# Two decoder layers: five steps of each mixer moved one feature later in TensorE's order

## The chip, the cores and the metric

One NeuronCore of a Trainium2 chip runs the whole kernel in one launch. The metric is the device time of one execution in microseconds; the time before is the median of three runs. The profile shown is of one execution, and its times count from the first instruction.

## What is computed

Two layers on 256 tokens of width 1024, all in float32. In each layer the tokens are projected, four mixers of width 256 work side by side, their results are joined and projected back, and a layer norm and a gated feed-forward follow. Cut to what matters here:

```python
def hybrid_mixer(x, w_in, b_forget, ...):
    z = x @ w_in
    aq, ak, av, bq, bk, bv, bf, cu, cv, dp = jnp.split(z, IN_SPLITS, axis=-1)
    ya = moba_attention(partial_rotary(aq), partial_rotary(ak), av)
    log_f = jax.nn.log_sigmoid(bf + b_forget)
    yb = forgetting_attention(bq, bk, bv, log_f)
    yc = causal_spatial_gating(gelu(cu), gelu(cv), ...)
    yd = multiscale_pool(dp, pool_w, pool_scale)
    return concatenate([ya, yb, yc, yd]) @ w_o

def forgetting_attention(q, k, v, log_f):
    c = jnp.cumsum(log_f, axis=-1)
    logits = q @ k.T * scale + c[..., :, None] - c[..., None, :]
    p = softmax(where(kpos <= qpos, logits, -inf))
    return p @ v
```

With 256 tokens and blocks of 256 the first attention is a plain causal softmax attention behind a rotation of the first 16 dimensions of each head. Both attentions have four heads of 64, worked on in pairs: index i = 0 and 1.

## The kernel before, in words

**Numbers.** A product of two float32 matrices is made of three products of rounded parts (float32r): high times high, high times low, low times high. So each weight is loaded (DMA on SyncE's queue, half a megabyte at a time), cast to its high part on ScalarE (L134, `wh`) and reduced to its low part on VectorE (L136, `wl`). This is called a split. `weights` (L142) asks for the splits of the unit that TensorE needs and of those up to `reach` units after it; there are 12 buffers for high parts, 10 for low ones.

**The mixer's steps.** `tokens` makes the values of both attentions, the gating branch and the forget gates with tokens on partitions. `feature(i, c)` (L453) makes a block of 128 features for all 256 tokens from one unit of weights: 8 x 3 products. Features 0 are the gating's, 1 the pooling's; 2 and 4 are queries and keys (c = 0, 1) of the first attention's head pairs 0 and 1, 3 and 5 those of the forgetting attention. Then:

- `forget_gates` (L397): a chain of small operations on VectorE that ends in the copies into `nlx`. `cumulate` (L418) sums them over the tokens by four products with a triangle (L420, L421); ScalarE copies rows of the sum into `fq` and `fk`.
- `rotary(i, z)` (L468): ScalarE copies the feature (`zrot`), VectorE multiplies it by cosines (`qk`) and shuffles the copy (`swp`), GpSimd multiplies that by sines (L477), VectorE adds it into `qk`.
- `forget(i, z)` (L482): ScalarE copies queries and keys into `fq` and `fk`. `pick_heads` (L202) prepares the other rows of these on GpSimd (L206, L207) for a head pair.
- `pooling`, `pool_means`: sums over windows on GpSimd. `pool_out` (L574): products (L577), ScalarE scales, and `result` splits into `yh` and `yl`.
- `scores(mx, i)` (L491): products of queries and keys (L507) of mixer mx (0 the first attention, from `qk`; 1 the forgetting one, from `fq` and `fk`) and their softmax: two reductions a head on VectorE into `pr`, exponentials on ScalarE, reciprocals and products on VectorE.
- `turned(mx, i)` (L521): transposes of `pr` on TensorE (L527), copied by ScalarE into `pt`. `values(mx, i)` (L533): products with the values (L539), then `result` (L319).
- `project(kt, ...)` (L585): the joint projection (L595 to L597) of one block of 128 features of the result.

**What sets the order.** TensorE's order is the order of the program, written out in L599 to L660 (manual schedule). The other engines' orders are set by a scheduler, when the program is built: by priority, earlier lines first, filling idle time with whatever is ready, splits above all. Each engine then works its list in order. The steps are `urgent` (L264): their instructions get a higher priority, and those on VectorE and ScalarE are queued behind the last recorded instruction of the urgent steps before:

```python
def urgent(f):
    def g(*a, **k):
        with ExitStack() as es:
            es.enter_context(tc.high_priority(offset=URGENT))
            for e in ORDERED:
                if recent[e] is not None:
                    es.enter_context(tc.issue_after(recent[e].ins))
            return f(*a, **k)
    return g
```

All recorded instructions are issued from one helper, so the profile shows them as L257, told apart by their tiles.

Of the kernel before, what the change touches and what calls it, by code (L numbers as in the profile page):

```python
# [24 lines left out]
SCALE = HD ** -0.5  # L25
# [31 lines left out]
def hybrid_block(ctx, tc, x, xT, wA1, wA3, wZ, wO, wU, wD, lnp, vecs, sguwT, sgub, scalep, convp, poolw, consts, out):  # L57
# [18 lines left out]
    mask = cst[:, CW_MASK:CW_MASK + 256]  # L76
    neghalf = cpool.tile([P, 4], F32, name="neghalf")

# [1 line left out]
    stream = []  # L80
    index = {}

# [25 lines left out]
    behind = [None]  # L108
# [37 lines left out]
            split_one()  # L146
        return units[i]

# [1 line left out]
    xTh = cpool.tile([P, NKT, S], F32R, name="xTh")  # L150
    xTl = cpool.tile([P, NKT, S], F32R, name="xTl")
    x_sb = [None, None]
# [15 lines left out]
        nc.scalar.copy(xTh[:, ks, :], xv)  # L168
        nc.vector.tensor_sub(xTl[:, ks, :], xv, xTh[:, ks, :].bitcast(F32))

    # the array's clock rises with a few microseconds of work: products of zeros while the first loads run
    idle = apool.tile([P, 512], F32, tag="w2", name="idle", bufs=W2).bitcast(BF16)[:, 0:512]
    nc.vector.memset(idle, 0.0)
    warm = psum()
    first = load_xT(0, 1)
# [16 lines left out]
        for o, e in ((CW_WIN, CW_TRI), (CW_TRI, CW), (CW_COS, CW_WIN)):  # L192
            nc.sync.dma_start(cst[:, o:e], consts[:, o:e])

    # forgetting attention: q k + (c_q - c_k) / SCALE as one product over a head's 64 rows and, in the other 64,
    # (1 / SCALE at the head's row | -c) times (-c | -1 / SCALE at the head's row)
    nlx = cpool.tile([P, 2, P], F32, name="nlx")
    nc.gpsimd.memset(nlx, 0.0)
    fq = [cpool.tile([P, S], F32, name=f"fq{h}") for h in range(2)]
# [47 lines left out]
    recent = {"vector": None, "scalar": None}  # L247

    class Recorded:
        """An engine whose last instruction is kept, for the stages that follow to queue behind it."""  # L250

        def __init__(self, name):
            self.name, self.engine = name, getattr(nc, name)
# [19 lines left out]

    @urgent
    def layer_norm(m, acc, ln, final):
        """x = LN(alpha x + acc) of 128 tokens; returns what transposes half of it for the products to come."""
        r = x_sb[m]
        last = final and m == 1
        spans = THREE if last else HALVES
        step = 256 if last else 512  # L280
        st = apool.tile([P, 4, 6], F32, tag="lnst", name="lnst")
        for o, w in spans:
            vector.scalar_tensor_tensor(r[:, o:o + w], r[:, o:o + w], ALPHA, acc[o][:, :w],
                                        op0=ALU.mult, op1=ALU.add)
            for c in range(o, o + w, step):
                vector.bn_stats(st[:, c // step, :], r[:, c:c + step])
        mv = apool.tile([P, 4], F32, tag="mv", name="mv")
        vector.bn_aggr(mv[:, 0:2], st[:, :DM // step, :].rearrange("p a b -> p (a b)"))
        nc.gpsimd.tensor_scalar(mv[:, 2:3], mv[:, 1:2], LN_EPS, None, op0=ALU.add)  # L289
        nc.gpsimd.tensor_tensor(mv[:, 3:4], mv[:, 2:3], neghalf[:, 0:1], op=ALU.pow)  # L290
        for n in range(2):
            ns = slice(512 * n, 512 * n + 512)
            vector.scalar_tensor_tensor(r[:, ns], r[:, ns], mv[:, 0:1], ln[:, 0, ns],
                                           op0=ALU.subtract, op1=ALU.mult)
        for i, (o, w) in enumerate(spans):
            ns = slice(o, o + w)
            behind[0] = vector.scalar_tensor_tensor(r[:, ns], r[:, ns], mv[:, 3:4], ln[:, 1, ns],
                                                    op0=ALU.mult, op1=ALU.add)
            if final:
                (nc.sync, nc.scalar)[i % 2].dma_start(out[m * P:(m + 1) * P, ns], r[:, ns])  # L300

        @urgent
        def turn(n):
            tp = psum()
            for k in range(4):
                nc.tensor.transpose(tp[:, k * P:(k + 1) * P], r[:, 512 * n + k * P:512 * n + (k + 1) * P], ident)
            tv = tp.rearrange("p (k t) -> p k t", k=4)
            ks, ms = slice(4 * n, 4 * n + 4), slice(m * P, (m + 1) * P)
            scalar.copy(xTh[:, ks, ms], tv)
            vector.tensor_sub(xTl[:, ks, ms], tv, xTh[:, ks, ms].bitcast(F32))  # L310

        return turn

    def mixer(l, norm2):
# [2 lines left out]
        yT = {}  # L317

        def result(kt, src):  # L319
            """Splits a block of the mixers' joint result, features on partitions, for the projection."""  # L320
            yh = apool.tile([P, S], F32R, tag="yh", name="yh", bufs=YB)
            yl = apool.tile([P, S], F32R, tag="yl", name="yl", bufs=YB)
            scalar.copy(yh, src)
            vector.tensor_sub(yl, src, yh.bitcast(F32))
            yT[kt] = (yh, yl)

        # tokens on partitions: values of both attentions, the gating branch, the forget gates
        V, VN = [], []
        zf = apool.tile([P, 2, 4], F32, tag="zf", name="zf")

# [59 lines left out]
            for r in held + tokens("A1", (1,)) + tokens("A3", (1,)):  # L390
                token_results(*r)

        # log_sigmoid(z) = min(z, 0) - 2 atanh(w / (2 + w)), w = exp(-|z|)
        zz = zf.rearrange("p m h -> p (m h)")

        @urgent
# [20 lines left out]
        @urgent  # L417
        def cumulate():  # L418
            ps = psum()
            nc.tensor.matmul(ps[:, :S], nlx[:, 0, :], tri, start=True, stop=False)  # L420
            nc.tensor.matmul(ps[:, P:S], nlx[:, 1, :], tri[:, 0:P], start=False, stop=True)  # L421
            for hh in range(2):
                o = HD - HD * hh
                scalar.copy(fk[hh][o:o + 32, :], ps[o:o + 32, :S])
                scalar.copy(fq[hh][o + 32:o + HD, :], ps[o + 32:o + HD, :S])

        # gating: mix the tokens of each chunk, features on partitions
        gate_u = {}

        @urgent  # L430
# [30 lines left out]
                nc.tensor.matmul(a, wh, xTl[:, k, :], start=False, stop=False)  # L461
                nc.tensor.matmul(a, wl, xTh[:, k, :], start=False, stop=(k == NKT - 1))  # L462

        # attention: queries and keys, scores, weights transposed, values, transposed result
        att = {}

        @urgent
# [21 lines left out]

        @urgent  # L490
        def scores(mx, i):  # L491
            """Heads 2i, 2i+1 of mixer mx: negated logits, masked, and their softmax over the keys."""
            t = att[mx, i]
            nm = apool.tile([P, 2, 2], F32, tag="nm", name="nm")
            sm = apool.tile([P, 2, 2], F32, tag="sm", name="sm")
            spans = ((0, P), (P, 2 * P))
            t["pr"] = []
            for hh in range(2):
                if mx == 0:
                    rows = slice(hh * HD, (hh + 1) * HD)  # L500
                    q, k = t["qk"][rows, 0, :], t["qk"][rows, 1, :]
                else:
                    q, k = fq[hh], fk[hh]
                ps = psum()
                pr = apool.tile([P, 384], F32, tag="pr", name="pr", bufs=4)
                for m, (o, n) in enumerate(spans):
                    nc.tensor.matmul(ps[:, o:o + n], q[:, m * P:(m + 1) * P], k[:, 0:n], start=True, stop=True)  # L507
                for m, (o, n) in enumerate(spans):
                    vector.tensor_tensor_reduce(out=pr[:, o:o + n], in0=ps[:, o:o + n], in1=mask[:, 2 * P - n:],
                                                   op0=ALU.add, op1=ALU.min, scale=-SCALE, scalar=3e38,  # L510
                                                   accum_out=nm[:, hh, m:m + 1])
                for m, (o, n) in enumerate(spans):
                    scalar.activation(pr[:, o:o + n], pr[:, o:o + n], AF.Exp, bias=nm[:, hh, m:m + 1],
                                         scale=-1.0, accum_out=sm[:, hh, m:m + 1])
                vector.reciprocal(sm[:, hh, :], sm[:, hh, :])
                for m, (o, n) in enumerate(spans):
                    vector.tensor_scalar(pr[:, o:o + n], pr[:, o:o + n], sm[:, hh, m:m + 1], None, op0=ALU.mult)
                t["pr"].append(pr)
# [43 lines left out]

        @urgent
        def pool_means():
            """A window's sum less the window's size times the token; the size divides after the product."""
            po = pool["po"]
            nc.gpsimd.tensor_mul(d["scale"], d["scale"], means)
            for i, total in enumerate(pool["sums"]):
                rows, g = slice(i % 2 * HD, (i % 2 + 1) * HD), i // 2
                nc.gpsimd.tensor_mul(total[rows, 16:32], total[rows, 16:32], start[rows, g, :])  # L570
                nc.gpsimd.tensor_sub(po[rows, g, :], total[rows, 16:], po[rows, g, :])  # L571
# [27 lines left out]
        both = (0, 1)  # L599
# [12 lines left out]
        if norm2 is None:  # L612
            load_x()
        gating()
        cumulate()
        feature(3, 1)
        forget(0, 3)
        scores(0, 0)
        feature(4, 0)
        scores(1, 0)  # L620
        feature(4, 1)
        turned(0, 0)
        pick_heads(1)
        rotary(1, 4)
        pool_out()
        feature(5, 0)
        values(0, 0)
        turned(1, 0)
        feature(5, 1)
        forget(1, 5)  # L630
        values(1, 0)
        scores(0, 1)
        reach[0] = HIGHS - 1
        project(4, both)
        scores(1, 1)
        project(5, both)
        turned(0, 1)
# [242 lines left out]
```

## Time and profile before

| | |
|---|---|
| median of 3 runs | 586.87 us (585.36 to 587.61) |
| profiled execution, first to last instruction (span) | 583.9 us; its time as the runs count it is not recorded |
| mean granted TensorE clock | 0.990 of full |
| TensorE products busy | 563.0 us (96%) |
| VectorE, ScalarE, GpSimd busy | 445.5 (76%), 323.9 (55%), 80.9 us (14%) |
| HBM read | 105.16 MB |

PE is TensorE, DVE VectorE, ACT ScalarE, POOL GpSimd, SP SyncE. A TensorE that is busy 96% of the span can only be made faster where it stands still or runs at a lower clock; both are found by stage, not in the sums. The first mixer's features run from about 25 to 72 us, the second's from about 311 to 357 us.

### The profile page before, as it was taken

The numbers are of one execution on the slowest core, as the hardware profiler recorded it, in microseconds if no ns is written. First come the engines' busy times: TensorE is split into PE (matmuls) and PEld (weight loads), VectorE is DVE, ScalarE is ACT, GpSimd is POOL, SyncE is SP. The second block draws the span as 40 slices with busy tenths as digits, with TensorE's granted clock in tenths as the row PEclk, the third lists the DMA queues.
The fourth block names the chain that finished last, engine by engine and source line by source line (L and its number), as shares of the span: only waits on it lengthen the run. The fifth ranks groups of instructions, "written<-read, shape, count | busy, mean of one in ns | idle before, by whom it ended". The sixth has DMA issues, their size and how long they took to land.

```text
span 583.9 us, 10273 instructions
## 1 busy us (share of the span) xinstructions
PE 563.0 (96%) x3962; PEld 515.2 (88%) x3962; DVE 445.5 (76%) x781; ACT 323.9 (55%) x539; POOL 80.9 (14%) x104
## 2 busy tenths in 40 slices
PE   7997999999999999999999989999999999999994
PEld 4996877899899999999789978779999999999994
DVE  4688985988877777678898868488886777767756
ACT  5774972386655555555548468435764555555420
POOL 2186431100000000000117730020000000000002
PEclk9998999999999999999999989999999999999998
DMA  8976871485555554445468624318656655544101
GB/s 284 336 259 211 282 269 70 160 309 185 199 194 181 181 184 176 146 150 177 150 207 312 226 73 133 134 36 319 222 183 186 201 188 180 182 148 152 63 1 72
DMA packets 31473, 106.88 MB, mean 183 GB/s; under 512 B 3776, under 2 KB 5184, under 8 KB 30912
## 3 DMA queue, kind: packets, MB, share of 16 engines
q1 hardware_dynamic: 31136, 105.83, 53.8%
q8 instruction: 31, 0.51, 0.4%
q10 hardware_dynamic: 288, 0.39, 0.2%
q14 instruction: 18, 0.15, 0.1%
HBM read 105.16 MB, written 1.05 MB: 182 GB/s over the span
## 4 chain that ended last, share of the span: by engine, by line
PE 77%; POOL 8%; DVE 8%; DMA 3%; issue 2%; ACT 1%; SPq 0%; POOLq 0%; DVEq 0%; ACTq 0%
PE ps L706 13%; PE ps L705 13%; PE ps L704 13%; PE ps L740 6%; PE ps L738 6%; PE ps L739 6%; DVE x L257 2%; PE ps L595 2%; PE ps L597 2%; PE ps L596 2%; DVE wl L136 2%; PE ps L340 2%; PE ps L341 1%; DVE lnst L257 1%; POOL po L571 1%
## 5 line engine op out<-in xcount | busy, mean ns | idle before, releaser
L136 DVE TENSOR_TENSOR wl<-wr,wh 128x1024 fp32r<-128x1024 f32 (+2 forms) x185 | 225.3, 1225 | 64.2 <-PE ps L706 41.2
L134 ACT CAST wh<-wr 128x1024 fp32r<-128x1024 f32 (+2 forms) x185 | 191.1, 1043 | 116.1 <-PE ps L705 58.1
L704 PE MATMUL ps<-xTh,wh 128*128 128x256 f32 x640 | 179.6, 281 | 0.0
L706 PE MATMUL ps<-xTh,wl 128*128 128x256 f32 x640 | 179.3, 280 | 0.0
L705 PE MATMUL ps<-xTl,wh 128*128 128x256 f32 x640 | 179.3, 280 | 0.0
L705 PEld LDWEIGHTS ps<-xTl,wh 128*128 128x128 f32 x640 | 120.6, 188 | 1.0
L704 PEld LDWEIGHTS ps<-xTh,wh 128*128 128x128 f32 x640 | 120.4, 188 | 1.0
L706 PEld LDWEIGHTS ps<-xTh,wl 128*128 128x128 f32 x640 | 120.6, 188 | 0.0
L257 DVE SCALAR_TENSOR_TENSOR cva<-ps,conv,cva 128x255 f32<-128x255 f32 (+1 forms) x176 | 84.5, 480 | 18.8 <-ACT cva L257 15.6
L257 ACT ACTIVATE cva<-ps,conv 128x256 f32<-128x256 f32 x88 | 49.5, 562 | 43.8 <-DVE cva L257 42.2
L738 PE MATMUL ps<-wh,gh 128*128 128x512 f32 (+1 forms) x198 | 73.3, 370 | 0.0
L740 PE MATMUL ps<-wh,gl 128*128 128x512 f32 (+1 forms) x198 | 73.2, 370 | 0.0
L739 PE MATMUL ps<-wl,gh 128*128 128x512 f32 (+1 forms) x198 | 73.1, 369 | 0.0
L289 POOL TENSOR_SCALAR mv<-mv 128x1 f32<-128x1 f32 x8 | 6.3, 782 | 423.5 <-DVE mv L257 423.5
L460 PE MATMUL ps<-xTh,wh 128*128 128x256 f32 x192 | 56.5, 294 | 0.0
L461 PE MATMUL ps<-xTl,wh 128*128 128x256 f32 x192 | 55.1, 287 | 0.0
L462 PE MATMUL ps<-xTh,wl 128*128 128x256 f32 x192 | 55.1, 287 | 0.0
L740 PEld LDWEIGHTS ps<-wh,gl 128*128 128x128 f32 x198 | 37.2, 188 | 6.9
L739 PEld LDWEIGHTS ps<-wl,gh 128*128 128x128 f32 x198 | 37.3, 188 | 5.8
L738 PEld LDWEIGHTS ps<-wh,gh 128*128 128x128 f32 x198 | 37.2, 188 | 5.7
L460 PEld LDWEIGHTS ps<-xTh,wh 128*128 128x128 f32 x192 | 37.7, 197 | 0.8 <-issue 0.7
L461 PEld LDWEIGHTS ps<-xTl,wh 128*128 128x128 f32 x192 | 37.6, 196 | 0.1
(126 smaller groups left out, 735.9 us busy)
## 6 DMA issues: line engine op xcount, KB each, us to landing
wr<-in_wU_dram SPq DMA_DIRECT2D x88, 512.0 KB, 3.8
wr<-in_wD_dram SPq DMA_DIRECT2D x44, 512.0 KB, 3.4
wr<-in_wZ_dram SPq DMA_DIRECT2D x24, 512.0 KB, 4.9
wr<-in_wO_dram SPq DMA_DIRECT2D x16, 512.0 KB, 4.4
lnp<-in_lnp_dram SPq DMA_DIRECT2D x4, 1024.0 KB, 5.5
wr<-in_wA_dram SPq DMA_DIRECT2D x7, 512.0 KB, 3.5
wr<-in_wA_dram SPq DMA_DIRECT2D x4, 520.0 KB, 4.4
x<-in_x_dram SPq DMA_DIRECT2D x4, 256.0 KB, 4.7
```

What stands on the lines that cost most here:

```text
L134: nc.scalar.copy(h[:, ps], raw[:, ps])
L136: nc.vector.tensor_sub(lo[:, ps], raw[:, ps], h[:, ps].bitcast(F32))
L257: ins = getattr(self.engine, op)(*a, **k)
L460: nc.tensor.matmul(a, wh, xTh[:, k, :], start=(k == 0), stop=False)
L461: nc.tensor.matmul(a, wh, xTl[:, k, :], start=False, stop=False)
L462: nc.tensor.matmul(a, wl, xTh[:, k, :], start=False, stop=(k == NKT - 1))
L704: nc.tensor.matmul(a, wh, xTh[:, k, :], start=(k == 0), stop=False)
L705: nc.tensor.matmul(a, wh, xTl[:, k, :], start=False, stop=False)
L706: nc.tensor.matmul(a, wl, xTh[:, k, :], start=False, stop=(k == NKT - 1))
L738: nc.tensor.matmul(a, gh[:, t], h[:, c], start=(j == 0), stop=False)
L739: nc.tensor.matmul(a, gh[:, t], lo[:, c], start=False, stop=False)
L740: nc.tensor.matmul(a, gl[:, t], h[:, c], start=False, stop=(j == NPAIR - 1))
```

## The change

In both mixers `cumulate` and `scores(0, 0)` move behind `feature(4, 0)`; `rotary(1, 4)` and `pool_out` come before `scores(1, 0)`, which moves behind `feature(4, 1)`; `pick_heads(1)` stays behind `scores(1, 0)`; `turned(0, 0)` moves behind `feature(5, 0)`, `values(0, 0)` and `turned(1, 0)` behind `feature(5, 1)` and `forget(1, 5)`, and `values(1, 0)` behind `project(4)`. The order of the features and projections among themselves stays. The diff's other parts only remove comments.

```diff
@@ -612,26 +612,26 @@
         if norm2 is None:
             load_x()
         gating()
-        cumulate()
         feature(3, 1)
         forget(0, 3)
+        feature(4, 0)
+        cumulate()
         scores(0, 0)
-        feature(4, 0)
-        scores(1, 0)
         feature(4, 1)
-        turned(0, 0)
-        pick_heads(1)
         rotary(1, 4)
         pool_out()
+        scores(1, 0)
+        pick_heads(1)
         feature(5, 0)
+        turned(0, 0)
+        feature(5, 1)
+        forget(1, 5)
         values(0, 0)
         turned(1, 0)
-        feature(5, 1)
-        forget(1, 5)
-        values(1, 0)
         scores(0, 1)
         reach[0] = HIGHS - 1
         project(4, both)
+        values(1, 0)
         scores(1, 1)
         project(5, both)
         turned(0, 1)
```

## Rows read from the trace of the kernel before

**Rows 1.** Waits of TensorE in the first mixer (19 to 100 us): engine line, releaser: us in total, times, longest
```profile
PE ps L420 <- issue: 3.4, 1, 3.4
PE ps L507 <- DVE qk L257: 1.0, 2, 0.7
```

**Rows 2.** Windows, TensorE alone: stretch, length, PE busy (instructions), granted clock, DMA share, GB/s
```profile
27.61:30.45 2.84, 2.84 (x27) 1.00 0.96 330
49.60:54.21 4.61, 4.61 (x27) 0.63 0.42 133
339.41:343.87 4.46, 4.46 (x27) 0.62 0.23 71
```

**Rows 3.** Timeline of TensorE, second mixer: start us, us, what, count [idle before <-releaser]
```profile
338.55 0.93 PE L507 MATMUL ps<-qk 64*128 64x128 f32 x8 [2.55 <-DVE qk L257]
...
343.87 1.47 PE L507 MATMUL ps<-fk,fq 128*128 128x128 f32 x8
...
353.27 0.88 PE L527 MATMUL ps<-cst,pr 128*128 128x128 f32 x6
...
356.91 0.87 PE L539 MATMUL ps<-pt,v 128*64 128x256 f32 x8
```

**Rows 4.** Chain of work that ended last, first mixer: start us, us, what
```profile
30.21 1.68 POOL gv L374
...
52.03 1.99 POOL swp L477
```

**Rows 5.** Timeline of TensorE, first mixer
```profile
54.87 0.93 PE L507 MATMUL ps<-qk 64*128 64x128 f32 x8 [0.66 <-DVE qk L257]
...
58.71 1.58 PE L507 MATMUL ps<-fk,fq 128*128 128x128 f32 x8
...
68.49 1.26 PE L527 MATMUL ps<-cst,pr 128*128 128x128 f32 x6
72.49 0.87 PE L539 MATMUL ps<-pt,v 128*64 128x256 f32 x8
```

**Rows 6.** Windows, VectorE alone: stretch, length, DVE busy (instructions), granted clock, DMA share, GB/s
```profile
54.03:73.55 19.52, 18.32 (x48) 1.00 0.86 288
```

**Rows 7.** Windows of the splits on VectorE (L136) alone, same columns
```profile
54.03:69.26 15.23, 8.47 (x7) 1.00 0.84 273
54.03:73.55 19.52, 9.69 (x8) 1.00 0.86 288
```

**Rows 8.** Waits of ScalarE, 60 to 110 us, columns as in rows 1
```profile
ACT wh L134 <- PE ps L597: 12.1, 3, 8.8
```

**Rows 9.** Timeline of ScalarE, second mixer
```profile
342.62 0.37 ACT L257 COPY fk<-ps 64x256 f32<-64x256 f32 x1
343.01 1.05 ACT L134 CAST wh<-wr 128x1024 fp32r<-128x1024 f32 x1
```

**Rows 10.** Timeline of VectorE, second mixer
```profile
346.06 0.90 DVE L257 TENSOR_SCALAR pr<-pr,sm 128x128 f32<-128x128 f32 x2
...
348.01 0.28 DVE L257 CUSTOM_DVE_ANT_0 pr<-ps,cst 128x128 f32<-128x128 f32 x1
...
350.43 0.55 DVE L257 TENSOR_SCALAR pr<-pr,sm 128x128 f32<-128x128 f32 x2
...
352.54 0.69 DVE L257 TENSOR_TENSOR qk<-ps,cst 128x512 f32<-128x512 f32 x1 [0.42 <-ACT zrot L257]
...
353.15 0.75 DVE L257 STREAM_SHUFFLE swp<-zrot 128x512 f32<-128x512 f32 x1
355.37 0.69 DVE L257 TENSOR_TENSOR qk<-qk,swp 128x512 f32<-128x512 f32 x1 [1.47 <-POOL swp L477]
355.98 0.76 DVE L257 TENSOR_TENSOR yl<-yd,yh 128x256 fp32r<-128x256 f32 x2
```

**Rows 11.** Timeline of GpSimd: L477 of rotary(1, 4) in the first and the second mixer
```profile
70.69 2.14 POOL L477 TENSOR_TENSOR swp<-swp,cst 128x512 f32<-128x512 f32 x1 [6.28 <-DVE swp L257]
...
354.05 1.29 POOL L477 TENSOR_TENSOR swp<-swp,cst 128x512 f32<-128x512 f32 x1 [5.25 <-DVE swp L257]
```

## The prediction

> **What bounds the kernel now.** I read the page of the profile first: in a span of 583.9 us TensorE is busy for 563.0. Its order is written out by hand, so only two things can be won by moving steps: time in which it stands still, and time in which it runs at half clock. The view of TensorE's waits over the first mixer shows two standstills: 3.4 us at `cumulate` (L420) and 1.0 us in two waits for `qk` at `scores` [rows 1]. The windows show the second loss: a whole `feature` takes 2.84 us at a granted clock of 1.00, but the one after each long wait took 4.61 and 4.46 us, at 0.63 and 0.62, so part of it ran at 1.2 instead of 2.4 GHz: 1.8 and 1.6 us lost [rows 2]. The timeline of the second mixer shows one long wait, 2.55 us for `qk` at `scores(0, 0)` [rows 3]; at `cumulate` there is none. All standstills and slow stretches of both mixers together are 3.42 + 0.66 + 0.34 + 2.55 + 1.8 + 1.6 = 10.4 us, the most that could be gained.
>
> The chain of waits then tells who is late. In the first mixer it runs over GpSimd from 30.21 us to the `sin` product L477, which begins at 52.03 and takes 1.99, and from there over VectorE's sum into `qk` to `scores(0, 0)` at 54.87 [rows 4, 5]. So the wait at `cumulate` is not what the chain hangs on: had TensorE not waited there, it would have waited for `qk`. Behind that sum VectorE, which works in order, is full: from 54.03 to 73.55 it is busy 18.32 of 19.52 us, and 9.69 of these are eight splits of weights (L136) [rows 6, 7].
>
> **The change, part by part.** No instruction is added or removed. The features keep their order, and with it every weight load on SyncE's queue and the place where each split is asked for; the splits are far ahead (ScalarE's casts wait up to 8.8 us for TensorE to free a buffer [rows 8]), so an earlier feature finds its weights. I cost the loads at nothing; if that cover were gone, one late weight would hold TensorE for a cast and a split, 1.05 + 1.21 = 2.3 us [rows 7, 9].
>
> *Part 1, `cumulate` and `scores(0, 0)` behind `feature(4, 0)`.* First mixer: the 3.4 us at `cumulate` go, since two features now stand there. But without that wait and the slow stretch `feature(3, 1)` and `cumulate`, which only change places, are done at 54.87 - 0.66 - 3.42 - 1.8 = 49.0, and `feature(4, 0)` at 51.8. `scores(0, 0)` is reached then and stands until 54.87, because nothing on GpSimd or VectorE ahead of `qk` is touched. The wait is 3.0 us long, near that of before, and a half-clock stretch behind it is likely again. What is won at this point is one feature, 2.84 us. Second mixer: the hole of 2.55 us is filled with `feature(4, 0)`, and `scores(0, 0)` begins at 338.55 - 2.55 + 2.84 = 338.84, without a wait. Won here: the hole, 2.55 us, and the 1.6 us of clock.
>
> *Part 2, `rotary(1, 4)` and `pool_out` ahead of `scores(1, 0)`.* Here is the price. Each urgent step queues its VectorE and ScalarE work behind that of the step before. Today the softmax of `scores(1, 0)` follows that of `scores(0, 0)`; after the change the product, shuffle, wait for GpSimd's L477 and sum of `rotary(1, 4)`, and the two `yl` of `pool_out`, stand between: 0.69 + 0.75 + 0.69 + 0.76 us and the GpSimd trip [rows 10]. `turned(1, 0)`, which needs the result, is now followed on TensorE by `scores(0, 1)` and the whole projection.
>
> When does TensorE reach `turned(1, 0)`? Before, from the start of `scores(1, 0)` to `turned(1, 0)` stand 9.78 us in the first mixer and 9.40 in the second [rows 3, 5]. After the change the same steps and `feature(5, 1)` (2.84) lie between the end of `scores(0, 0)` (0.93 after its start) and it: 55.8 + 12.62 = 68.4, and 339.8 + 12.24 = 352.0. The last copy into `fk` ends at 342.99 in the second mixer [rows 9], 4.4 us behind the start of `scores(0, 0)`; `feature(4, 1)` and `pool_out` take about as long, so `scores(1, 0)` finds its inputs.
>
> When are the weights of `scores(1, 0)` ready? First mixer, by VectorE's own sum: 18.32 - 9.69 = 8.63 us of work that must be done from 54.03 on, plus the two `yl` (0.76) that came after it: 9.4. With each split 1.21 us and k of them let in: 54.03 + 9.4 + 1.21 k. Today seven were let in before the last normalisation of `scores(1, 0)`, which ends at 69.26 [rows 7]; I take 7, which gives 71.9. Second mixer: the softmax of `scores(0, 0)` ends at 346.96; product and shuffle 1.4; L477; sum 0.69; `yl` 0.76; then 2.97 from the first reduction to the last normalisation (348.01 to 350.98) [rows 10]. L477 took 1.29 us with VectorE idle and 2.14 with a split beside it [rows 11]; splits will fill this wait, so I take 2.1: 354.9.
>
> So TensorE waits some 3 us at `turned(1, 0)` in each mixer. Its second half then takes 0.44 us (half of 0.88 [rows 3]), and `scores(0, 1)` starts at 72.3 and 355.3. The same point of work before, with `values(1, 0)` not yet done, was 72.49 + 0.34 = 72.8 and 356.91. Gain: 0.5 and 1.6 us. Bounds: in the first mixer k from 5 (gain 2.9) to 8 with 1.2 us of idle VectorE as today (loss 2.0); in the second from 3.5 (the cast of 1.05 us not ahead of the exponentials [rows 9], L477 at 1.29) to 0.4 (one more split).
>
> About L477 the Trainium skill (SBUF — State Buffer, section "SBUF: two separate sides") says that VectorE with two SBUF inputs and GpSimd hold a shared port by an exclusive lock, so that the later one blocks for the whole instruction. By that an L477 behind a split would take up to 1.29 + 1.21 = 2.5 us, an estimate, and the second mixer would gain 1.2 instead of 1.6 and the sum be 586.9; the measured 2.14 is below it, and I keep 2.1.
>
> *Part 3, the clock.* Waits of 3.42 and 2.55 us were each followed by half clock; those of 0.66 and 0.34 were not. The waits at `turned(1, 0)` come in two pieces with transposes between, and in the first mixer a slow stretch behind `scores(0, 0)` makes TensorE arrive 1.7 us later and the wait shorter. I count one half-clock stretch for the two mixers, 1.7 us, with 0 and 3.4 as ends.
>
> *The rest.* `values(0, 0)` and `turned(0, 0)` find their inputs (in the second mixer the softmax ends at 346.96 and `turned(0, 0)` is reached at about 347.4; in the first it has the same distance). `values(1, 0)` behind `project(4)` has its transposes copied during that projection. `scores(0, 1)` no longer waits for `qk` (0.34, already counted). `pick_heads(1)` on GpSimd moves behind L477 in program order; its next reader, `scores(1, 1)`, is over 3 us away. From 0 to 1 us if a PSUM buffer is late at `project(4)`; I take 0.
>
> Sum: 0.5 + 1.6 - 1.7 = 0.4 us faster. The profiled execution's span is 583.9, the median of the runs 586.87, 3.0 above it; I take the difference from the median: **586.5 us**. Own range of this case, from its bounds: 584.0 to 589.5.
>
> **Rivals.** *Faster: the softmax is in time.* If few splits are let in (k = 5) and no cast stands ahead of the exponentials, the gains are 2.9 and 3.5, the waits at `turned(1, 0)` fall to about 1 us and no half clock follows: 580.5 at its end, 582.5 as its middle. For it: in the second mixer L477 did run at 1.29, with VectorE idle beside it. Against it: VectorE's 94% in the first.
>
> *Slower: the softmax of `scores(1, 0)` behind rotary's GpSimd trip becomes the bound.* If eight splits and today's idle stand ahead of it in the first mixer (-2.0), one split more in the second (+0.4), and both waits end in half clock (-3.4): 587 + 5 = 592 at its end, 590.5 in its middle. It decides once TensorE stands at `turned(1, 0)` for over about 4 us in the first mixer. For it: VectorE has no slack there. Against it: TensorE then has two more features behind it.
>
> *The change does nothing in the end:* `qk` bounds the first mixer on both sides and the second's gain goes into one half-clock stretch; 586.9, inside the forecast's band.
>
> **Chances.** What a measurement of this kernel can tell from no change is about 0.5%, 2.9 us. Faster by more 0.30 (the first rival and the forecast's good end), within it 0.45 (the forecast 0.38, the last rival 0.07), slower by more 0.25. As both outer cases hold more than a tenth, the range reaches to their middles: 581.5 to 590.5.
>
> **What would show it.** Right: TensorE's wait at L420 gone in the first mixer, a wait of about 3 us at L507 for `qk` in its place; no wait at L507 in the second mixer; new waits at L527 for `pr`, 1.5 to 3.5 us in each; the `pr` rows of `scores(1, 0)` on VectorE behind the two `yl` of `pool_out`. Wrong: `pr` ready before TensorE comes (gain then up to the hole itself), `qk` of the first mixer ready well before 54, or waits at `project(4)` for a PSUM buffer.

## The result, and the profile after

The changed kernel takes 595.12 us in the median of 4 runs (592.79 to 595.47), the kernel before 586.31 (now four runs, 585.36 to 587.61). By the medians it is slower by 8.8 us, and outside the predicted range. The ratio used from here on is formed from the single runs and not from the medians: 1.0141, with an interval of 1.0124 to 1.0158. The profiled execution has a span of 593.2 us, 9.3 above that of before.

The page of the changed kernel, its head: TensorE is busy for 2.3 us longer than before (563.0 us then); the other 7.0 of the 9.3 us are time in which it stands.

```profile
PE 565.3 (95%) x3962; PEld 514.7 (87%) x3962; DVE 446.2 (75%) x781; ACT 324.6 (55%) x539; POOL 81.6 (14%) x104
```

**Where it stands.** (In what follows, pair 0 and pair 1 are the two head pairs of the first attention, and half clock is a stretch with a granted clock of 0.50.) Call the stretch from the first product of `gating` (L443) to the first transposes of the layer norm (L306) a mixer stage; everything that the change moves lies in it. The first stage took 56.27 us before and takes 61.11 now (46.54 to 107.65), the second 53.50 and 55.83 (338.17 to 394.00): 4.84 + 2.33 = 7.2 of the 9.3 us. From the first stage's end to the second's start (230.5) and from the second's end to the last instruction (199.2) nothing differs by over 0.1. The other 2.1 us lie ahead of the first stage, where no step is moved (the last section comes back to them).

Waits of TensorE in the changed kernel, first mixer (44 to 110 us), then second (335 to 395), in the columns of [rows 1]:

```profile
PE ps L539 <- ACT pt L257: 5.7, 1, 5.7
PE ps L507 <- DVE qk L257: 2.8, 1, 2.8
PE ps L507 <- ACT fq L257: 0.8, 1, 0.8
...
PE ps L539 <- ACT pt L257: 3.5, 1, 3.5
PE ps L507 <- ACT fq L257: 0.5, 1, 0.5
```

Against [rows 1, 3], three things stand here. The 3.4 us at L420 are gone and 2.8 us at L507 for `qk` have come in their place; the 2.55 us for `qk` in the second mixer are gone; and there is a new wait in both mixers, at L539, the products of `values(0, 0)`, for `pt`: ScalarE's copy of the transposed weights. No wait stands at L527, the transposes of `turned(1, 0)`, where the prediction had put it.

TensorE's timeline of the changed kernel, first mixer ([rows 5] show the same lines before):

```profile
57.00 0.93 PE L507 MATMUL ps<-qk 64*128 64x128 f32 x8 [2.83 <-DVE qk L257]
...
67.02 0.91 PE L527 MATMUL ps<-cst,pr 128*128 128x128 f32 x6
...
76.46 1.92 PE L539 MATMUL ps<-pt,v 128*64 128x256 f32 x8 [5.74 <-ACT pt L257]
78.31 1.40 PE L527 MATMUL ps<-cst,pr 128*128 128x128 f32 x6
79.64 0.93 PE L507 MATMUL ps<-qk 64*128 64x128 f32 x8
```

The transposes of `turned(0, 0)` are done at 67.9. Their copies come eight microseconds later. ScalarE's timeline of the changed kernel says why:

```profile
74.18 0.40 ACT L257 ACTIVATE pr<-pr,nm 128x128 f32<-128x128 f32 x1 [0.86 <-DVE nm L257]
...
75.95 0.83 ACT L257 COPY pt<-ps 128x384 f32<-128x384 f32 x2
```

The copies of `turned(0, 0)` stand in ScalarE's list behind the exponentials of `scores(1, 0)`, and these wait for VectorE's minima `nm`. Before, those exponentials ran from 63.95 to 65.72 and the copies began at 66.78:

```profile
63.95 0.40 ACT L257 ACTIVATE pr<-pr,nm 128x128 f32<-128x128 f32 x1
...
66.78 0.86 ACT L257 COPY pt<-ps 128x384 f32<-128x384 f32 x2
```

VectorE's timeline of the changed kernel gives the rest, from the sum of pair 0 to the softmax of `scores(1, 0)`:

```profile
56.16 0.69 DVE L257 TENSOR_TENSOR qk<-qk,swp 128x512 f32<-128x512 f32 x1 [1.15 <-POOL swp L477]
...
59.91 4.63 DVE L136 TENSOR_TENSOR wl<-wr,wh 128x1024 fp32r<-128x1024 f32 x4
64.45 0.28 DVE L257 CUSTOM_DVE_ANT_0 pr<-ps,cst 128x128 f32<-128x128 f32 x1
...
67.62 1.23 DVE L136 TENSOR_TENSOR wl<-wr,wh 128x1024 fp32r<-128x1024 f32 x1 [0.19 <-ACT wh L134]
68.76 0.68 DVE L257 TENSOR_TENSOR qk<-ps,cst 128x512 f32<-128x512 f32 x1
...
69.37 0.75 DVE L257 STREAM_SHUFFLE swp<-zrot 128x512 f32<-128x512 f32 x1
70.01 1.21 DVE L136 TENSOR_TENSOR wl<-wr,wh 128x1024 fp32r<-128x1024 f32 x1
72.38 0.69 DVE L257 TENSOR_TENSOR qk<-qk,swp 128x512 f32<-128x512 f32 x1 [1.16 <-POOL swp L477]
72.99 0.95 DVE L257 TENSOR_TENSOR yl<-yd,yh 128x256 fp32r<-128x256 f32 x2
73.86 0.28 DVE L257 CUSTOM_DVE_ANT_0 pr<-ps,cst 128x128 f32<-128x128 f32 x1
```

Two things are late. The softmax of `scores(0, 0)` begins at 64.45, though its products were done at 57.93; four splits went first. And between its last normalisation (67.43) and the first reduction of `scores(1, 0)` lie 6.43 us: product, shuffle, GpSimd's trip, sum and two `yl`, with two splits. Before, it was 1.1 us (62.57 to 63.63), with one split:

```profile
61.35 1.22 DVE L257 TENSOR_SCALAR pr<-pr,sm 128x128 f32<-128x128 f32 x4
...
63.63 0.28 DVE L257 CUSTOM_DVE_ANT_0 pr<-ps,cst 128x128 f32<-128x128 f32 x1
```

In the second mixer the same wait has no full VectorE behind it (it idles 4.19 us ahead of the first sum). ScalarE, second mixer, changed kernel:

```profile
360.26 0.40 ACT L257 ACTIVATE pr<-pr,nm 128x128 f32<-128x128 f32 x1 [2.80 <-DVE nm L257]
...
362.03 0.83 ACT L257 COPY pt<-ps 128x384 f32<-128x384 f32 x2
```

Here ScalarE idles 2.80 us for `nm`, and TensorE stands 3.51 us for the copy that follows.

### The profile page after: what moved, and what is told of

It reads as the page before. It is cut to its first block, busy times and chain, and to the rows that moved or that the text cites. A ratio compares the mean times of both kernels' runs of the same rounds, so it can differ in the third digit from the quotient of the medians.

```text
span 593.2 us, 10279 instructions
## 1 busy us (share of the span) xinstructions
PE 565.3 (95%) x3962; PEld 514.7 (87%) x3962; DVE 446.2 (75%) x781; ACT 324.6 (55%) x539; POOL 81.6 (14%) x104
## 4 chain that ended last, share of the span: by engine, by line
PE 70%; DVE 11%; POOL 9%; ACT 3%; issue 3%; DMA 2%; SPq 0%; POOLq 0%; DVEq 0%; ACTq 0%
PE ps L705 13%; PE ps L706 13%; PE ps L704 13%; PE ps L740 6%; PE ps L738 6%; PE ps L739 6%; DVE wl L136 4%; DVE x L257 3%; PE ps L595 2%; PE ps L597 2%; PE ps L596 2%; DVE lnst L257 2%; PE ps L539 1%; ACT wh L134 1%; POOL po L571 1%
## 5 line engine op out<-in xcount | busy, mean ns | idle before, releaser
L136 DVE TENSOR_TENSOR wl<-wr,wh 128x1024 fp32r<-128x1024 f32 (+2 forms) x185 | 224.3, 1221 | 68.7 <-PE ps L706 39.8
L705 PEld LDWEIGHTS ps<-xTl,wh 128*128 128x128 f32 x640 | 120.6, 188 | 1.0
L704 PEld LDWEIGHTS ps<-xTh,wh 128*128 128x128 f32 x640 | 120.4, 188 | 1.0
L706 PEld LDWEIGHTS ps<-xTh,wl 128*128 128x128 f32 x640 | 120.6, 188 | 0.0
L460 PEld LDWEIGHTS ps<-xTh,wh 128*128 128x128 f32 x192 | 36.1, 188 | 1.1 <-issue 1.0
L462 PEld LDWEIGHTS ps<-xTh,wl 128*128 128x128 f32 x192 | 36.2, 189 | 0.0
```

The lines of the kernel that those rows point to most:

```text
L136: nc.vector.tensor_sub(lo[:, ps], raw[:, ps], h[:, ps].bitcast(F32))
L460: nc.tensor.matmul(a, wh, xTh[:, k, :], start=(k == 0), stop=False)
L704: nc.tensor.matmul(a, wh, xTh[:, k, :], start=(k == 0), stop=False)
```

## The experiments

Theory A: what was put ahead of `scores(1, 0)`, that is the work of `rotary(1, 4)` and `pool_out` on VectorE, GpSimd and ScalarE, delays its softmax, and TensorE waits behind that. Theory B: the softmax of `scores(0, 0)`, a feature later and behind four splits, is what delays all. Theory C: only ScalarE's order does it, with the copies `pt` behind the exponentials.

A measure that the clock of TensorE disturbs little serves through all of them: in the first mixer, the time from the start of VectorE's sum into `qk` of pair 0 to the first reduction of `scores(1, 0)`, and to the first copy `pt` of `turned(0, 0)`. Beside it stand TensorE's waits at or behind `values(0, 0)` and `turned(1, 0)`.

| kernel | ratio to before | first reduction of (1, 0) | first copy `pt` (0, 0) | wait for `pt` or `pr`, first and second mixer |
|---|---|---|---|---|
| before | 1 | 9.60 | 12.75 | none |
| changed | 1.0141 | 17.70 | 19.79 | 5.74, 3.51 |
| e1: rotary and pool_out back | 1.0026 | 12.59 | 16.91 | 2.17, 1.07 |
| e2: copies first | 1.0152 | 17.73 | 17.05 | 3.98, 3.67 |
| e4: part 2 alone | 1.0101 | 16.79 | 19.83 | 4.01, 1.08 |
| e5: splits behind softmax | 1.0162 | 17.65 | 19.74 | 4.28, 4.35 |
| e6: e1 and e5 | 1.0048 | 12.25 | 16.27 | 1.54, 0.43 |
| e9: rotary back | 1.0100 | 14.40 | 17.86 | 3.59, 1.64 |
| e10: pool_out back | 1.0171 | 16.98 | 21.34 | 5.72, 2.91 |
| e11: sum and pool_out back | 1.0038 | 13.84 | 18.20 | 3.45, 0.73 |

**e1.** The later places of `cumulate` and all of pair 0 stay; `rotary(1, 4)` and `pool_out` go back behind `scores(1, 0)`.

```diff
         feature(4, 1)
-        rotary(1, 4)
-        pool_out()
         scores(1, 0)
         pick_heads(1)
+        rotary(1, 4)
+        pool_out()
         feature(5, 0)
```

> The changed kernel with rotary(1, 4) and pool_out back behind scores(1, 0) and pick_heads(1), all else as changed. Theory A (VectorE's softmax of scores(1, 0) comes late because rotary, its GpSimd trip and pool_out stand ahead of it): the long waits at L539 (5.73 and 3.51 us) fall under 1.5 us, the time to 585 to 588 us. Theory B (the four splits that the planner puts ahead of the softmax of scores(0, 0) are the cause): the first mixer stays late, a wait of 3 us or more at L539 or L527 is left there, 590 to 593 us.

587.96 us (587.30 to 589.71), ratio 1.0026 [1.0007, 1.0044]. Waits of TensorE in e1, first mixer, then second:

```profile
PE ps L507 <- DVE qk L257: 3.8, 2, 2.8
PE ps L539 <- ACT pt L257: 2.2, 1, 2.2
PE ps L507 <- ACT fq L257: 1.7, 1, 1.7
...
PE ps L507 <- ACT fq L257: 1.7, 1, 1.7
PE ps L539 <- ACT pt L257: 1.1, 1, 1.1
```

The waits at L539 fall from 5.7 to 2.2 and from 3.5 to 1.1 us, though four splits still stand ahead of the softmax of `scores(0, 0)` (4.63 us from 58.60, its first reduction at 63.14). Both stages together take 5.4 us less than in the changed kernel (111.6 against 116.9). About half of that is time in which TensorE stands (11.3 us against 14.0) and half is clock, as e1 has no half clock in the stages. The first wait stays over the 1.5 us that A had been given. Still, two steps moved back return most of the loss: for A.

**e2.** TensorE's order stays that of the changed kernel; the softmax of `scores(1, 0)` is issued behind `turned(0, 0)`, so that ScalarE copies `pt` first.

```diff
         feature(5, 0)
         turned(0, 0)
+        softmax(1, 0)
         feature(5, 1)
```

> The changed kernel with TensorE's order untouched; only the softmax of scores(1, 0) is written behind turned(0, 0), so that ScalarE copies the transposes of turned(0, 0) before the exponentials of scores(1, 0). Theory C (the wait at values(0, 0) comes from ScalarE's queue, the copies stand behind exponentials that wait): the waits at L539 fall by 2 us or more in each mixer and the time with them, 588 to 591 us. Theory A (the late softmax itself is the bound): the waits at L539 get shorter, but the same time is waited one step on, at the transposes L527 of turned(1, 0); 593.5 to 596 us.

596.58 us (594.61 to 597.34), ratio 1.0152 [1.0118, 1.0185], just above A's range. Waits of TensorE in e2, first mixer, then second (L506, L538 and L550 are its lines of `scores`, `turned` and `values`):

```profile
PE ps L506 <- DVE qk L257: 2.8, 1, 2.8
PE ps L538 <- DVE pr L257: 2.5, 2, 1.8
PE ps L550 <- ACT pt L257: 1.5, 1, 1.5
...
PE ps L538 <- DVE pr L257: 3.7, 2, 2.9
```

Most of the wait leaves the values' products and comes back at the next step, the transposes that need `pr` of `scores(1, 0)`: 7.7 us in both mixers where there were 9.2, with more half clock behind them (20.5 us in the two stages for 6.8). ScalarE's order decides where TensorE stands more than for how long, and the time is no better. How much of the half clock belongs to this order is open, so take the time that the stretch as a whole needs, clock included: from the sum of pair 0 to `scores(0, 1)`, with the same TensorE work between, the changed kernel takes 23.48 and 21.32 us in the two mixers, e2 23.04 and 20.73, e1 20.51 and 18.42. C is worth 1.0 us of this, A 5.9: C falls as the main cause.

**e3 and e4.** One half of the change each, made from the kernel before and from the changed one.

```diff
# e3: the kernel before with part 1 alone
         gating()
-        cumulate()
         feature(3, 1)
         forget(0, 3)
-        scores(0, 0)
         feature(4, 0)
+        cumulate()
+        scores(0, 0)
         scores(1, 0)
# e4: the changed kernel without part 1
         gating()
+        cumulate()
         feature(3, 1)
         forget(0, 3)
-        feature(4, 0)
-        cumulate()
         scores(0, 0)
+        feature(4, 0)
         feature(4, 1)
```

> The kernel before with one move alone: cumulate and scores(0, 0) behind feature(4, 0). Theory A (the harm is in the second part): 581.5 to 586 us, the second mixer's wait at L507 gone with its slow stretch, the first mixer's moved from L420 to L507. Theory B (moving scores(0, 0) back lets splits in ahead of its softmax): 587 to 591 us, new waits at L527 in the first mixer.

> The changed kernel with cumulate and scores(0, 0) back in their old places; the rest stays changed (rotary(1, 4) and pool_out ahead of scores(1, 0), the turned and values steps late). Theory A: 590 to 596 us, waits at L539 of 3 to 6 us in both mixers. Theory B: 585 to 588 us.

e3: 591.59 us (590.80 to 592.42), ratio 1.0078 [1.0051, 1.0106]. e4: 593.19 (592.17 to 593.31), ratio 1.0101 [1.0076, 1.0127]. e3 is above the ranges of both theories. Its waits of TensorE, first mixer, then second:

```profile
PE ps L507 <- ACT fq L257: 4.7, 1, 4.7
PE ps L507 <- DVE qk L257: 2.9, 1, 2.9
...
PE ps L507 <- ACT fq L257: 4.6, 1, 4.6
```

In e3 `scores(1, 0)` follows `cumulate` and `scores(0, 0)` with no feature between, and TensorE stands 4.7 and 4.6 us for the copies into `fq`. So e3 costs time by a wait that the full change does not have (0.8 and 0.5 us there): part 1 needs the later place of `scores(1, 0)`, and e3 prices neither theory. e4 is the cleaner one. Its softmax of `scores(0, 0)` begins 4.89 us behind the sum (59.44 to 54.55), just as before (58.92 to 54.03). Its softmax of `scores(1, 0)` begins 16.79 us behind it all the same: the splits that no longer go ahead of the first softmax (two behind the sum instead of five) go behind it (five instead of two). A late first softmax isn't needed: B falls for the most part. Not altogether, as the wait in the second mixer is 1.08 us here, not the 3 to 6 that A expected.

**e5 and e6.** B by itself: from `feature(4, 1)` on, splits are queued behind the softmax of `scores(0, 0)`, in the changed kernel (e5) and in e1 (e6).

```diff
         scores(0, 0)
+        behind[0] = recent["vector"]
         feature(4, 1)
```

> The changed kernel with one line more: from feature(4, 1) on, the splits asked for are queued on VectorE behind the softmax of scores(0, 0), so that one split instead of four stands between the gating branch's yl and that softmax in the first mixer. Theory B as a part of the cause (each of the three splits ahead of the softmax is 1.15 us late for everything behind it): the first mixer is shorter by 2 to 4 us, 590 to 593 us. Theory A alone (rotary and pool_out): no change beyond 1 us, 594 to 596 us.

> Both at once: rotary(1, 4) and pool_out behind scores(1, 0) as in e1, and the splits queued behind the softmax of scores(0, 0) as in e5; cumulate, scores(0, 0), the turned and values steps stay as late as the change put them. If A and B together are the whole loss: 583 to 586 us, waits at L539 under 1 us in both mixers. If something else is left in the late steps: 587 to 589 us, as e1.

e5: 594.66 us (593.79 to 598.38), ratio 1.0162 [1.0121, 1.0203]. e6: 589.12 (587.37 to 591.04), ratio 1.0048 [1.0031, 1.0066]. VectorE's timeline of e5, first mixer:

```profile
58.15 1.22 DVE L136 TENSOR_TENSOR wl<-wr,wh 128x1024 fp32r<-128x1024 f32 x1
59.29 0.28 DVE L257 CUSTOM_DVE_ANT_0 pr<-ps,cst 128x128 f32<-128x128 f32 x1
...
62.64 0.17 DVE L257 RECIPROCAL sm<-sm 128x2 f32<-128x2 f32 x1 [2.16 <-ACT pr L257]
...
64.34 2.54 DVE L136 TENSOR_TENSOR wl<-wr,wh 128x1024 fp32r<-128x1024 f32 x2
```

One split stands ahead of the softmax instead of four, and its reductions run 4.88 us behind the sum. But VectorE then idles 2.16 us for the exponentials: ScalarE still has its copies of `forget` and `cumulate` ahead of them. The splits put off go right behind it, ahead of rotary's product. The first reduction of `scores(1, 0)` comes 17.65 us behind the sum, as without the fence (17.70), and in e6 12.25, as in e1 (12.59). In the first mixer the splits only filled time that would have been waited anyway. Of the medians this says less, as e5 has a stretch of half clock behind L507 that the changed kernel lacks (last section); TensorE reaches `values(0, 0)` 1.4 us later for it, and so its wait there is shorter (4.28 us). e6, at 589.12, is just above its upper range. It waits less for `pt` than e1, but then stands 2.15 us for `qk` at `scores(0, 1)` in each mixer.

**e9, e10, e11.** Theory A taken apart, all from the changed kernel: only `rotary(1, 4)` behind `scores(1, 0)` (e9), only `pool_out` (e10), `pool_out` and rotary's last step, the sum that waits for GpSimd (e11).

```diff
# e9
-        rotary(1, 4)
         pool_out()
         scores(1, 0)
         pick_heads(1)
+        rotary(1, 4)
# e10
         rotary(1, 4)
-        pool_out()
         scores(1, 0)
         pick_heads(1)
+        pool_out()
# e11: rotary(1, 4) without its sum
         rotary(1, 4)
-        pool_out()
         scores(1, 0)
         pick_heads(1)
+        add_sines(1)
+        pool_out()
```

> The changed kernel with rotary(1,4) alone behind scores(1,0) again; pool_out stays ahead of them, and TensorE's order is that of the changed kernel to the last product. Theory A (the VectorE and GpSimd work of rotary stands ahead of the softmax of scores(1,0), and the values wait for it): the product 0.61, the shuffle 0.64, the 1.16 us of waiting for GpSimd and the sum 0.61 go from ahead of it, some 3.0 us in the first mixer and 2.3 in the second; the wait at the values' products falls from 5.7 to about 2.7 and from 3.5 to about 1.2; 589 to 591. Theory P (pool_out, with its products, two scalings, two casts and two yl ahead, is what costs): 593.5 to 595.5.

> The changed kernel with pool_out alone behind scores(1,0) again; rotary(1,4) stays ahead. Theory A: only two yl of 0.87 us in all go from ahead of the softmax of scores(1,0), and the scalings and casts from ScalarE's list; 1.0 to 2.0 us over both mixers: 593 to 594.5. Theory P: 588 to 590.

> The changed kernel, but of rotary(1,4) only the sum (which waits for GpSimd's product) and pool_out stand behind scores(1,0); its copy, product and shuffle stay ahead. If the trip through GpSimd is the larger part of theory A, this gains the 1.16 us of waiting, the sum 0.61 and pool_out's two yl 0.87 in the first mixer and about as much in the second, 4.5 to 5.5 us in all: 589.5 to 591. If the product and the shuffle with the casts around them are the larger part: 592.5 to 594.

e9: 592.21 us (591.32 to 593.84), ratio 1.0100 [1.0072, 1.0129]. e10: 596.89 (595.89 to 597.89), ratio 1.0171 [1.0146, 1.0196]. e11: 588.81 (587.26 to 590.74), ratio 1.0038 [1.0022, 1.0053]. All three lie outside what was written, on one side or the other: the parts don't add. Read in pairs they do tell. e10 and e11 differ in rotary's sum alone, and by 8.1 us. VectorE where the softmax of `scores(1, 0)` begins, in e10:

```profile
67.92 0.75 DVE L257 STREAM_SHUFFLE swp<-zrot 128x512 f32<-128x512 f32 x1
68.57 1.20 DVE L136 TENSOR_TENSOR wl<-wr,wh 128x1024 fp32r<-128x1024 f32 x1
70.96 0.69 DVE L257 TENSOR_TENSOR qk<-qk,swp 128x512 f32<-128x512 f32 x1 [1.19 <-POOL swp L477]
71.56 0.28 DVE L257 CUSTOM_DVE_ANT_0 pr<-ps,cst 128x128 f32<-128x128 f32 x1
```

And in e11:

```profile
69.21 0.76 DVE L257 STREAM_SHUFFLE swp<-zrot 128x512 f32<-128x512 f32 x1
69.84 0.28 DVE L257 CUSTOM_DVE_ANT_0 pr<-ps,cst 128x128 f32<-128x128 f32 x1
```

From the shuffle to the first reduction it is 3.64 us with the sum between (a split, 1.19 us of idleness for GpSimd's product, the sum) and 0.63 without. That is 3.0 us in the first mixer; the waits at `values(0, 0)` fall by 2.3 and 2.2 us (5.72 to 3.45, 2.91 to 0.73). Most of the rest goes with the clock in the profiled executions: e10 shows 17.1 us of half clock in its stages, e11 3.4, and TensorE is busy there for 106.8 and 101.7 us.

e1 and e9 differ in `pool_out` alone, by 4.2 us, of which, in the profiled executions, 1.1 are standing in the two stages and 2.4 longer products: with it ahead, its scalings, casts and `yl` and a split hold the softmax back by 1.8 us (14.40 against 12.59), and e9 has 6.8 us of half clock where e1 has none. Yet in e10 moving `pool_out` back gains nothing. The softmax there begins 0.7 us earlier, but a cast slips between its exponentials, and `pool_out`'s four ScalarE instructions (1.3 us, 74.61 to 75.92) lie between them and the copies `pt`, which come 1.55 us later than in the changed kernel. The product and shuffle of rotary alone (e1 against e11) hold the softmax back by 1.25 us; the medians, 0.9 apart, don't tell them from nothing. So the sum and `pool_out` each gain when the other is already behind; `pool_out` by itself gains nothing, and the sum moved back with `pool_out` left ahead was not run.

**e7, e8, e12.** A version that beats both kernels was looked for where both still wait: `qk` of pair 0. In the kernel before, L477 of `rotary(0, 2)` stands on GpSimd behind nine small operations of `pool_means`. e7 is the kernel before with these behind L477. e8 takes e6, puts `forget_gates` and both pooling steps behind `rotary(0, 2)`, `scores(0, 0)` ahead of `cumulate`, and lets the sum of pair 0 go outside the queueing of urgent steps. e12 is e7 with `feature(4, 0)` ahead of `scores(0, 0)` and `feature(4, 1)` ahead of `scores(1, 0)`.

```diff
# e7
         rotary(0, 2)
-        pool_means()
+        with tc.issue_after(sines[0].ins):
+            pool_means()
# e12, on e7
-        scores(0, 0)
         feature(4, 0)
-        scores(1, 0)
+        scores(0, 0)
         feature(4, 1)
+        scores(1, 0)
```

> The kernel before, TensorE's order untouched; GpSimd's pool_means is queued behind the sine product L477 of rotary(0, 2). Theory: the start of scores(0, 0) is set by GpSimd's list, not by TensorE's order. Then the second mixer's wait at L507 (2.55 us) and its slow stretch go and the first mixer changes by under 1.5 us: 581.5 to 584.5 us. If the softmax chain behind it is the bound anyway: 585.5 to 587 us, new waits at L527 or L539.

> An attempt that uses what the runs showed, on top of e6: forget_gates is written behind rotary(0, 2), the sum into qk is free of the queueing, pooling and pool_means stand behind L477 on GpSimd, and cumulate stands one place behind scores(0, 0). If GpSimd's list and the splits held the mixers: 575 to 582 us, no wait over 1 us at L507 in either mixer. If VectorE's load in the first mixer is the bound: 582 to 586 us, waits at L527 or L539 there.

> The kernel before with the pooling means behind rotary's product on GpSimd (583.8 in its own run), and besides feature(4,0) ahead of scores(0,0) and feature(4,1) ahead of scores(1,0); the cumulation stays in its place. Theory A: the 1.7 us that TensorE waits for the sum in the first mixer is filled by feature(4,0), and the softmax of scores(1,0) stays ahead of rotary: 582 to 584.5. Rival (every softmax a feature later meets the splits and the values wait): 585 to 588.

e7: 583.81 us (582.44 to 585.53), ratio 0.9951 [0.9929, 0.9973]: faster than both. e8: 589.35 (588.04 to 590.08), ratio 1.0047 [1.0033, 1.0061]. e12: 586.74 (585.78 to 587.87), ratio 1.0002 [0.9988, 1.0016]. GpSimd's timeline, second mixer, before:

```profile
336.41 1.26 POOL L477 TENSOR_TENSOR swp<-swp,cst 128x512 f32<-128x512 f32 x1
```

And in e7:

```profile
333.75 2.16 POOL L477 TENSOR_TENSOR swp<-swp,cst 128x512 f32<-128x512 f32 x1 [0.75 <-DVE swp L257]
```

Counted from the start of the stage (331.22 and 333.31), L477 begins 0.4 us in instead of 5.2. No wait of over 0.25 us is left in the second stage and no half clock; it takes 49.38 us instead of 53.50. The first takes 57.18 instead of 56.27: there L477 waits 3.78 us for VectorE's shuffle, and GpSimd's order wins little. What it wins is lost again: the pooling products now run on GpSimd from 53.76 to 59.75, beside VectorE's work for the first softmax, and that takes longer. The two `yl` of the gating branch, in e7:

```profile
57.33 1.83 DVE L257 TENSOR_TENSOR yl<-yc,yh 128x256 fp32r<-128x256 f32 x2
```

And before:

```profile
57.11 0.75 DVE L257 TENSOR_TENSOR yl<-yc,yh 128x256 fp32r<-128x256 f32 x2
```

The splits on either side of them took 1.76 and 1.75 us, where before they took 1.22. So the softmax of `scores(0, 0)` begins 7.08 us behind the sum instead of 4.88. e8 missed: its gates came so late (the copies into `nlx` begin at 58.15, 48.77 in e7) that TensorE stood 5.55 us at `cumulate`. e12 came out in the range of its rival, and shows the price of theory B where it is real: in the first mixer three splits (4.23 us) go ahead of the softmax of `scores(0, 0)`, on top of work as long as in e7, so that it begins 9.56 us behind the sum; TensorE, with only one feature between that step's products and the transposes, stands at `turned(0, 0)`. Its timeline in e12 (the row names no releaser; VectorE's first normalisation for it ran from 65.26):

```profile
65.65 1.75 PE L527 MATMUL ps<-cst,pr 128*128 128x128 f32 x6 [5.27 <-issue]
```

## Why the prediction was wrong

The mechanism on record as the slower rival is the one that came: "the softmax of `scores(1, 0)` behind rotary's GpSimd trip becomes the bound". It had a chance of 0.25 and 592 us at its end; the measured 595.12 lies beyond that, and TensorE stands one step earlier than the rival said. Step by step:

- **Part 1 held.** The wait at L420 is gone; at L507 TensorE stands 2.83 us for `qk`, for 3.0 predicted; in the second mixer there is none for it. Left out were ScalarE's copies into `fq` and `fk` behind the later `cumulate`: `scores(1, 0)`, said to find its inputs, waits for them, 0.79 and 0.48 us.
- **"`values(0, 0)` and `turned(0, 0)` find their inputs": this step failed.** It looked at the softmax of `scores(0, 0)` alone. Between that and `values(0, 0)` stands ScalarE's copy `pt`, and the same rule of urgent steps that the prediction used for VectorE puts it behind the exponentials of `scores(1, 0)`. So TensorE stops one step earlier than predicted, with more work left behind the wait: `values(0, 0)` and all of `turned(1, 0)`, 3.18 us (76.46 to 79.64, at half clock) instead of half of `turned(1, 0)`, 0.44. That is 2.7 us more in the first mixer, and 2.9 in the second (362.54 to 365.86).
- **The sum for the softmax was too small.** Taken from the start of the `qk` sum, the weights were to be ready after 71.9 - 54.03 = 17.9 us, with k = 7. The last normalisation ended at 77.50, 21.3 us after it. One split more (1.2), 1.5 us of idleness on VectorE (1.16 of it at rotary's sum, [rows 6] have 1.2 in all) and 0.7 us more of VectorE's other work make the difference. The bound on record, eight splits and 1.2 us of idleness, gives 20.3 (and by its terms a loss of 1.9 us, not 2.0). TensorE was released by `pt` after 20.3 us, 2.4 later than predicted.
- **Together:** 2.4 + 2.7 = 5.1 us in the first mixer, where a gain of 0.5 was forecast and 4.84 was lost (0.2 is not placed). In the second, `pt` released TensorE at 362.54 - 6.95 = 355.6 on the scale of before (6.95 is by how much the stage starts later), 0.7 behind the predicted 354.9; with the 2.9 behind it that is 3.6, from a gain of 1.6 to a loss of 2.33 (0.3 is not placed). The 2.7 and 2.9 hold 1.2 and 1.3 us that the half clock costs, as the same products take 1.98 us in e1's second mixer at full clock. The forecast had 1.7 us for half clock as a term of its own, so the two sums lie 5.3 + 3.9 - 1.7 = 7.6 us apart: 0.4 won by the forecast, 7.2 lost in the two stages.
- **When TensorE arrives** was right to about a microsecond. It reached `values(0, 0)` at 70.72 - 2.11 = 68.6 on the scale of before; with 0.9 for those products that is 69.5 at `turned(1, 0)`, for 68.4 predicted, and 0.79 of the difference is the wait for `fq` at `scores(1, 0)`, which was said to find its inputs.
- **L477** took 2.08 us with a split beside it and 1.28 with VectorE idle, the values of [rows 11] to 0.06. In the second mixer no split came, so 2.1 was too much. By the Trainium skill's rule (SBUF — State Buffer, section "SBUF: two separate sides") the prediction had estimated up to 2.5 us, which is for a product that begins together with the split. Here it began 0.26 us behind it (70.27 and 70.01); blocked until the split's end at 71.22, it would have taken 0.95 + 1.28 = 2.23 us by that rule, an estimate, and the trace agrees to 0.15.
- **Part 3:** half clock came with the end of the wait at L539 in both mixers (76.02 to 79.44 and 362.74 to 366.15), two stretches where one was counted, as many as before. The slow stretch behind `scores(0, 0)` in the first mixer that was called likely did not come: the clock there was 1.00.
- **The loads** cost nothing, as said: in neither stage does TensorE wait over 0.15 us for a weight. But the 8.8 us of [rows 8] stand at 99.72, behind the features, and did not show that cover: at 45 to 50 us the casts waited 1.0 to 1.4 us for their loads.

Shown by the runs: that the steps ahead of `scores(1, 0)` make most of the loss (e1, and e4 with 1.0101 of the 1.0141), that within them the sum behind GpSimd's product and `pool_out` together carry most of it (e10 to e11, e9 to e1; each with the other already behind), and that ScalarE's order alone does not (e2). How the 3.0 us at rotary's sum divide between the idleness for GpSimd, the split let in there and the sum itself was read from the rows, not tried. What e1 still loses, 1.5 us by the ratio, was not taken apart: in its two stages TensorE stands 3.6 us longer than before, with 1.7 us for `fq` in each mixer that part 1 brings, and is busy 1.9 less, at full clock.

## What to carry to other kernels

A step moved to give its consumer more time moves its work on every engine that works its list in order; follow each queue to the next thing that TensorE needs, not only the result of the step itself. Here a copy that had been ready for eight microseconds waited behind exponentials that belonged to another step. A chain that leaves an engine and comes back (product, shuffle, GpSimd, sum) had better not stand ahead of a softmax that TensorE waits for: its last instruction holds the queue for the trip, and it can be moved behind by itself (e11, together with `pool_out`). And where a chain names an engine with small work ahead of a long-awaited product, as GpSimd here, putting that work behind was worth more than any move on TensorE tried here, 4.1 us in the second mixer; in the first the stage got 0.9 us longer, as VectorE's work beside it took longer.

## What was not expected of the hardware

A wait of TensorE of nearly one length at one place was followed by half clock in some profiles and not in others. Windows over all engines, behind the wait for `qk` at L507, in the changed kernel (wait 2.83 us):

```profile
57.00:61.85 4.85, 4.85 (x36) 4.06 (x36) 4.85 (x9) 3.91 (x8) 0.00 (x0) 1.00 0.94 312
```

And in e5 (2.84 us):

```profile
55.24:58.10 2.86, 2.86 (x14) 2.21 (x15) 2.86 (x7) 1.98 (x5) 0.00 (x0) 0.50 0.92 313
```

The granted clock, third from the end, is 1.00 (2.4 GHz) in one and 0.50 (1.2 GHz) in the other. Eight of these kernels have a wait of 2.82 to 2.86 us there: half clock followed in e2, e3, e5 and e10, none in the changed kernel, e1, e6 and e11. At this place the length of the wait does not tell, so a clock term of some 1.7 us [rows 2] is uncertain for each such wait, and experiments are better compared by waits and queue times than by medians alone. Where the waits differed more, their length did tell: ahead of `values(0, 0)`, in the kernels with the changed kernel's order from there on, half clock came with the end of all nine waits of 2.91 to 5.74 us or within 1.1 us of it, and with none of the seven of 0.43 to 2.17 us. So part of what e1, e9 and e11 win by a shorter wait there is probably clock.

The 2.1 us ahead of the first mixer are of this kind too: the changed kernel ran at half clock from 11.17 to 14.58 us, ahead of every moved step. e2, e3, e6 and e11 show such a stretch near 11 to 15 us, the kernel before and the others none, and their first gating products start at 46.3 to 46.9 us instead of 44.4 to 45.3. Whether the change has a part in how often it comes is open; the profiled execution of e5, without it, took 593.79 us, inside the changed kernel's 592.79 to 595.47.
